# Moving background steps: modulation around layer norm 0 on TensorE, table work behind the key activations, context job at one and two steps by turns

## The chip, the cores and the metric

The kernel runs on one core of a Trainium2 chip. The metric is the device time in microseconds (us) of one execution. A core has five engines, each with its own in-order queue: TensorE (PE, with its weight loads shown as PEld), VectorE (DVE), ScalarE (ACT), GpSimd (POOL) and SyncE (SP), which issues nearly all of the loads here. The engines wait for one another, and for DMA transfers, through semaphores.

## The reference

Two blocks follow each other on an activation of 256 tokens by 2048 features, all in float32. The first block has two layers. Layer 0 is a differential attention, layer 1 a forgetting attention with its own key/value projection; after each comes `x = layer_norm(ALPHA * x + gate * y)`. The input of each projection is modulated:

```
mod = c_act @ w_mod[l] + b_mod[l]
shift, scale, gate = jnp.split(mod, 3, axis=-1)
h = x * (1.0 + scale[:, None]) + shift[:, None]
```

The second block normalises x, modulates it with the same kind of vectors, and runs an S5 mixer (a complex linear recurrence over time, whose initial state comes from a context sequence of 256 tokens), a gated linear unit, and an MLP with a hidden size of 8192. The modulation vectors are products of one vector (for one of them two vectors) with large matrices: 224 chunks of 256 rows by 1024 columns, 1 MB each, every one read once.

## The kernel before, in words

**The projections.** x is held transposed, 16 tiles of 128 features by 256 tokens. A projection is a sequence of output tiles; `weights()` (L143) hands out the weights of one tile. Each tile is 1 MB, loaded by SP in two halves (L129), and split into a high and a low fp32r part by ACT (`wh`, L133) and DVE (`wl`, L134). `mm_t` (L152) and `mm_n` (L187) then run 48 matmuls: high by high, high by low, low by high. The high and low parts have five buffers each (`HL`), so that two and a half tiles can stand ready.

**Work in the background.** Each call of `weights()` also advances two kinds of other work.

- `bg()` (L292) takes the next chunk of the modulation queue `bgq`. It issues the two loads of the chunk (`graw`, L267, four buffers of 0.5 MB shared with the context's `wc` tiles and others) and runs the use of the chunk before it (`LATE = 1`). A use is either 8 matmuls on PE (L221) or two multiply-adds of 1024 columns on DVE (L236; the first one of an accumulation is an ACT multiply, L234). Which engine, or none, is read from a cyclic policy set for the stage (`P_ON0`, `P_KV` and so on); the two-vector chunks of `mc` always run on PE. After eight chunks a half of a vector is finished (L245 to L256). The queue's order is fixed by `JOBS`: m0, m02, mk, m1, mc, m12, m22, m24, m25.
- `step()` (L272) advances the first generator of `self.side` by one step, `next(self.steps)` times a call. Three such generators exist: the S5 input table, in layer 0; `s5_outputs_table` (L598), in the key/value stage, with two steps for each of 16 blocks; and `ctx_states` (L1297), which computes the final S5 state of the context in 8 blocks of five steps, after one step of preparation. The output table's first half-step makes products on DVE (L553, L554, L634, L636) and stores them; the second runs small matmuls (`kps`, L648) that need the loaded tile `gen_ws<-d_b` (L624). A context block has 128 small matmuls (`inc`, L695) and a scan of six levels on DVE (L1353 to L1356).

**The stages around the change.** Output projection 0 (`out_norm`, L1030) runs 16 tiles. After each, ACT multiplies by the gate (`yg`, L1089) and DVE adds the residual (L1090). From the tenth tile on, shifted copies (L1061), their squares (ACT, L1063) and sums on POOL (L1065 to L1068) gather the statistics; the last ones are summed by PE (L369). DVE then takes the root (L1108 to L1114), PE spreads mean and root over the partitions (L342). `layer1` (L1136) follows: `affine_split` (L411) walks through the 16 tiles of x; `norm(j)` is an add and a multiply on DVE (L1130, L1131), ACT applies scale and shift (L416) and makes the high part (`kH`, L418), DVE the low part (`kL`, L419). Directly behind it stand six modulation chunks (`BG_K`). The key/value stage then runs 32 tiles (keys: `mm_t`, copied out at L1201; values: `mm_n`), with the forget gate's small projection after the first. The query/gate stage runs two tiles for each of 16 heads, with the attention in between; from the fifth head on the context job runs beside it, and goes on in output projection 1. Behind that, `s5_mix` first completes the accumulation that DVE has open (`while self.open`, one chunk at a time), and then starts the S5 mixer.

**What sets the order.** The program text gives priorities. A planner (`schedule_with_timeline_sim`) goes through a modelled timeline and lays down each engine's order, ahead of the run: an instruction of later text is put before one of earlier text if its operands are there sooner in that model. At run time each engine follows its list. `issue_after(ins)` places the instructions of the block that are on the engine of `ins` behind `ins` in that list; those of other engines it leaves free.

Of the kernel before, what the change touches and what calls it, by code (L numbers as in the profile page):

```python
# [49 lines left out]
KO_K = 12  # L50
P_START = ("pe",)
P_L0A = ('dve', 'pe')
P_KV = ('dve', 'pe')
P_QG = ('dve', 'dve', 'pe')
P_W = ("pe",)
P_GLU = ('dve',)
P_MLP = ('dve', None, None)
P_ON0 = ('dve', 'dve', 'dve', None)
P_ON1 = ('pe', 'dve', None)
BG_V = 2  # L60
BG_W = 0
# [4 lines left out]
LATE = 1  # L66
NPJ = 4
INC = ('pj', 'pj')
BG_K = 6
BG_Q = 0  # L70
P_CTX = (1,)
HL = 5
JOBS = ("m0", "m02", "mk", "m1", "mc", "m12", "m22", "m24", "m25")
DVE_W = 2
# [7 lines left out]
E_K = "x"  # L82
# [23 lines left out]
class K:  # L106
# [164 lines left out]

    def step(self):  # L272

        while self.side and next(self.side[0], True):
            self.side.pop(0)

    def flush(self, job):
        while job in self.side:
# [132 lines left out]
    def affine_split(self, src, S, B, dst, js=range(KT)):  # L411

        nc = self.nc
        for j in js:
            u = self.tmp("u")
            nc.scalar.activation(u, src(j), AF.Identity, scale=S[:, j:j + 1], bias=B[:, j:j + 1])  # L416
            aH, aL = dst(j)
            nc.scalar.copy(aH, u)  # L418
            nc.vector.tensor_sub(aL, u, aH)  # L419

    def pair(self, name):
        H, L = self.act_tile(F32R, name + "H"), self.act_tile(F32R, name + "L")
# [278 lines left out]
    def run(self):  # L701
        tc, I = self.tc, self.I
        from contextlib import ExitStack
        with ExitStack() as es:
# [23 lines left out]
            self.steps = itertools.cycle((1,))  # L728
            self.open = False
            self.side = []  # L730
            self.x = xr.tile([128, KT, T], F32, name="xres")
            mod = lambda n: self.vt.tile([128, KT], F32, name=n)
            self.m0 = [mod(f"m0_{i}") for i in range(3)]
# [41 lines left out]
    def V(self, n):  # L775
        i = VEC[n] * KT
        return self.vecs[:, i:i + KT]
# [109 lines left out]
    def layer0(self):  # L887
# [114 lines left out]
        self.ctx_rms()  # L1002
        self.policy(P_ON0, X_ON0)
        self.norm = self.out_norm(o_, m0[2], 0)
# [131 lines left out]
    def layer1(self):  # L1136
        nc, V = self.nc, self.V
# [2 lines left out]
            self.bg_finish(n)  # L1140
        S, B = self.small_bg("lk", V("lg0"), self.mk[1], V("lb0"), self.mk[0])
        k_ = self.pair("k")
        self.affine_split(self.norm, S, B, k_)
        self.bg(BG_K, E_K)
        Fs = self.cp.tile([48, T], F32R, name="Fs")
        nid = self.cp.tile([48, 16], F32R, name="nid")
        FT = self.cp.tile([128, 2, 16], F32, name="FT")
# [1 line left out]
        def forget():  # L1149


            wz = self.t1.tile([128, KT, 16], F32, name="wz", tag="t1")
            nc.gpsimd.dma_start(wz, self.I["wz"])
            wzH = self.t1.tile([128, KT, 16], F32R, name="wzH", tag="t1")
            wzL = self.t1.tile([128, KT, 16], F32R, name="wzL", tag="t1")
            nc.scalar.copy(wzH, wz)
            nc.vector.tensor_sub(wzL, wz, wzH)
            zf = self.m.tile([16, T], F32, name="zf", tag="m")
            for kt in range(KT):
                aH, aL = k_(kt)  # L1160
                nc.tensor.matmul(zf, wzH[:, kt], aH, start=kt == 0, stop=False)
                nc.tensor.matmul(zf, wzH[:, kt], aL, start=False, stop=False)
                nc.tensor.matmul(zf, wzL[:, kt], aH, start=False, stop=kt == KT - 1)
            fz = self.t1.tile([16, T], F32, name="fz", tag="t1")
            fa = self.t1.tile([16, T], F32, name="fa", tag="t1")
            F = self.t1.tile([16, T], F32, name="F", tag="t1")
            nc.vector.tensor_scalar(fz, zf, self.bf[:, 0:1], None, op0=ADD)
            nc.scalar.activation(fa, fz, AF.Abs)
            nc.scalar.activation(fa, fa, AF.Tanh, scale=0.5)
            nc.vector.tensor_scalar(fa, fa, 0.5, 0.5, op0=MUL, op1=ADD)  # L1170
            nc.scalar.activation(fa, fa, AF.Ln)
            nc.vector.tensor_scalar(fz, fz, 0.0, None, op0=MIN)
            nc.vector.tensor_add(fa, fa, fz)
            nc.vector.tensor_tensor_scan(F, self.ones[:16].to_broadcast([16, T]), fa, 0.0, op0=MUL, op1=ADD)
            nc.scalar.mul(Fs, self.dm[:48, 0:T], 0.0)
            nc.scalar.copy(Fs[0:16], F)
            nc.vector.tensor_sub(Fs[32:48], F, Fs[0:16])
            nc.scalar.mul(nid, self.idn[:48, 0:16], 0.0)
            for i in (0, 32):
                nc.scalar.mul(nid[i:i + 16], self.idn[i:i + 16, i:i + 16], -1.0)  # L1180
            return F

        def forget_t(F):
            fp = self.m.tile([128, 2, 16], F32, name="fp", tag="m")
            for i in range(2):
                nc.tensor.transpose(fp[:, i], F[:, i * 128:i * 128 + 128], self.idn[:16, :16])
            nc.vector.tensor_copy(FT, fp)

        kT, v = [], []
        self.policy(P_KV, X_KV)  # L1190
        vgen = self.s5_outputs_table(self.act.tile([128, 4096], F32, name="gen2_ws", tag="act"))
        self.side.append(vgen)
        for j in range(32):
            if j == 1:
                F = forget()
            if j == 3:
                forget_t(F)
            if j < 16:
                ps = self.mm_t(k_)
                t = self.kv.tile([128, T], F32, name=f"k{j}", tag="kv")  # L1200
                with self.tc.issue_after(nc.scalar.copy(t, ps).ins):  # L1201
                    nc.scalar.activation(z[:, j], z[:, j], AF.Identity, scale=V("lg0")[:, j:j + 1],
                                         bias=V("lb0")[:, j:j + 1])
                kT.append(t)
            else:
                ps = self.mm_n(k_, j % 2)
                if j % 2:
                    for h in range(2):
                        t = self.kv.tile([128, 2, 128], F32, name=f"v{j - 17 + h}", tag="kv")
                        nc.scalar.copy(t, ps[:, :, h * 128:h * 128 + 128])  # L1210
                        v.append(t)
        self.flush(vgen)
        for i in (1, 0):
            self.bg_finish(f"m1_{i}")
        s1 = self.plus1("s1_1", self.m1[1])
# [50 lines left out]
        def start_ctx():  # L1266
            if self.ctx is None and not self.bg_open("mc_0") and not self.bg_open("mc_1"):
                Sc, Bc = self.small_bg("sc", V("mixpre"), self.mc[1], None, self.mc[0])
                self.ctx = self.ctx_states(Sc, Bc)
                self.side.append(self.ctx)  # L1270
                self.steps = itertools.cycle(P_CTX)

# [484 lines left out]
```

## Time and profile before

| | us |
|---|---|
| median of 3 runs | 2521.97 |
| lowest, highest | 2521.81, 2525.11 |
| profiled execution, its own time | 2525.04 |
| span of the profile (first to last instruction) | 2523.2 |

The page gives busy time by engine: PE 2337.6 us, DVE 1782.8, ACT 1196.4, POOL 174.5. The granted clock of PE is its share of full speed: 1.0 is 2.4 GHz, 0.5 is 1.2 GHz, a value between them is a mean over the stretch. Over the execution it was 0.95. Instructions of one engine may overlap by some tens of ns, so a sum of durations can exceed a stretch a little. In the views, a tile's name with an arrow (`out<-in`) tells what an instruction writes and reads, and what stands after `<-` behind an idle time is the event that ended it.

### The profile page before, as it was taken

The numbers are of one execution on the slowest core, as the hardware profiler recorded it, in microseconds if no ns is written. First come the engines' busy times: TensorE is split into PE (matmuls) and PEld (weight loads), VectorE is DVE, ScalarE is ACT, GpSimd is POOL, SyncE is SP. The second block draws the span as 40 slices with busy tenths as digits, with TensorE's granted clock in tenths as the row PEclk, the third lists the DMA queues.
The fourth block names the chain that finished last, engine by engine and source line by source line (L and its number), as shares of the span: only waits on it lengthen the run. The fifth ranks groups of instructions, "written<-read, shape, count | busy, mean of one in ns | idle before, by whom it ended". The sixth has DMA issues, their size and how long they took to land.

```text
span 2523.2 us, 49826 instructions
## 1 busy us (share of the span) xinstructions
PE 2337.6 (93%) x19814; PEld 2039.8 (81%) x19814; DVE 1782.8 (71%) x3357; ACT 1196.4 (47%) x2077; POOL 174.5 (7%) x255
## 2 busy tenths in 40 slices
PE   5699999999889999999998569899899999999997
PEld 1289999999778888988886457798788888888885
DVE  3278878887985555788788996897865665665655
ACT  0455445445365556555544443555544443443442
POOL 0000000000301111000000001232000000000000
PEclk8599999999889999999998779999899999999998
DMA  9999999887879998888786347997356555555652
GB/s 320 331 344 319 328 331 332 302 299 291 294 230 351 325 334 295 287 275 282 247 284 251 137 174 274 325 314 245 120 189 192 190 187 187 187 186 190 192 184 92
DMA packets 195450, 644.77 MB, mean 256 GB/s; under 512 B 32624, under 2 KB 41072, under 8 KB 194832
## 3 DMA queue, kind: packets, MB, share of 16 engines
q1 hardware_dynamic: 187744, 620.47, 71.9%
q0 software_dynamic: 7472, 21.11, 2.1%
q8 instruction: 155, 2.54, 0.4%
q14 instruction: 79, 0.65, 0.1%
HBM read 615.80 MB, written 25.69 MB: 254 GB/s over the span
## 4 chain that ended last, share of the span: by engine, by line
PE 76%; DVE 11%; DMA 8%; ACT 3%; issue 3%; SPq 0%; POOL 0%; DVEq 0%; ACTq 0%
PE pj L175 19%; PE pj L162 9%; PE pj L176 9%; PE pj L164 9%; PE pj L163 9%; DMA graw<-in_w_mod 6%; PE g L221 4%; PE pjv L199 3%; PE pjv L200 2%; PE pjv L201 2%; DVE gacc L236 2%; PE ko L1472 2%; DVE wl L134 1%; DVE scan_t L1428 1%; DVE S L1430 1%
## 5 line engine op out<-in xcount | busy, mean ns | idle before, releaser
L134 DVE TENSOR_TENSOR wl<-w,wh 128x1024 fp32r<-128x1024 f32 x631 | 779.3, 1239 | 433.5 <-ACT wh L133 421.7
L133 ACT CAST wh<-w 128x1024 fp32r<-128x1024 f32 x632 | 657.5, 1048 | 689.8 <-PE pj L175 279.9
L175 PE MATMUL pj<-h,wh 128*128 128x512 f32 x1024 | 361.9, 398 | 6.0 <-DVE h L419 4.2
L175 PE MATMUL pj<-d,wh 128*128 128x512 f32 x1024 | 358.4, 396 | 0.0
L236 DVE SCALAR_TENSOR_TENSOR gacc<-graw,csilu,gacc 128x1024 f32<-128x1024 f32 x200 | 267.8, 1339 | 42.4 <-DMA graw<-in_w_mod 37.8
L176 PE MATMUL pj<-h,wl 128*128 128x256 f32 x1024 | 287.4, 281 | 1.1 <-DVE wl L134 1.1
L176 PE MATMUL pj<-d,wl 128*128 128x256 f32 x1024 | 284.8, 279 | 0.0
L175 PEld LDWEIGHTS pj<-h,wh 128*128 128x128 f32 x1024 | 194.0, 189 | 53.4 <-issue 3.9
L175 PEld LDWEIGHTS pj<-d,wh 128*128 128x128 f32 x1024 | 191.9, 188 | 47.2 <-PE pj L176 1.7
L162 PE MATMUL pj<-hH,wh 128*128 128x256 f32 x768 | 221.4, 289 | 5.4 <-ACT hH L418 4.0
L164 PE MATMUL pj<-hH,wl 128*128 128x256 f32 x768 | 221.3, 289 | 0.5 <-DVE wl L134 0.5
L163 PE MATMUL pj<-hL,wh 128*128 128x256 f32 x768 | 221.0, 288 | 0.0
L221 PE MATMUL g<-graw,czc 128*32 128x256 f32 x1840 | 170.0, 451 | 46.3 <-DMA graw<-in_w_mod 43.9
L176 PEld LDWEIGHTS pj<-h,wl 128*128 128x128 f32 x1024 | 194.7, 190 | 1.5 <-DVE wl L134 1.5
L176 PEld LDWEIGHTS pj<-d,wl 128*128 128x128 f32 x1024 | 192.8, 188 | 0.4
L162 PEld LDWEIGHTS pj<-hH,wh 128*128 128x128 f32 x768 | 148.8, 194 | 8.9 <-ACT hH L418 4.1
L164 PEld LDWEIGHTS pj<-hH,wl 128*128 128x128 f32 x768 | 148.6, 194 | 4.5 <-issue 3.3
L163 PEld LDWEIGHTS pj<-hL,wh 128*128 128x128 f32 x768 | 148.8, 194 | 3.8 <-issue 3.7
L162 PE MATMUL pj<-h1H,wh 128*128 128x256 f32 x512 | 147.1, 290 | 1.4 <-DVE ws L1286 1.4
L163 PE MATMUL pj<-h1L,wh 128*128 128x256 f32 x512 | 146.3, 287 | 0.0
L164 PE MATMUL pj<-h1H,wl 128*128 128x256 f32 x512 | 145.4, 285 | 0.0
L221 PEld LDWEIGHTS g<-graw,czc 128*32 128x32 f32 x1840 | 48.8, 117 | 119.4 <-DMA graw<-in_w_mod 92.4
(483 smaller groups left out, 5120.5 us busy)
## 6 DMA issues: line engine op xcount, KB each, us to landing
graw<-in_w_mod SPq DMA_DIRECT2D x384, 512.0 KB, 6.1
w<-in_mlp_in SPq DMA_DIRECT2D x128, 512.0 KB, 3.7
w<-in_mlp_out SPq DMA_DIRECT2D x128, 512.0 KB, 3.9
w<-in_a_in SPq DMA_DIRECT2D x96, 512.0 KB, 6.1
graw<-in_w_kvmod SPq DMA_DIRECT2D x64, 512.0 KB, 6.1
w<-in_b_in SPq DMA_DIRECT2D x64, 512.0 KB, 5.9
w<-in_glu SPq DMA_DIRECT2D x56, 512.0 KB, 6.0
w<-in_a_v SPq DMA_DIRECT2D x32, 512.0 KB, 5.9
```

The source lines that it names most:

```text
L133: nc.scalar.copy(h, src)
L134: (eng or (nc.gpsimd if next(self.spl) else nc.vector)).tensor_sub(l, src, h)
L162: self.nc.tensor.matmul(ps, h, aH, start=kt == order[0] and not opened, stop=False)
L163: self.nc.tensor.matmul(ps, h, aL, start=False, stop=False)
L164: self.nc.tensor.matmul(ps, l, aH, start=False, stop=kt == order[-1] and last)
L175: self.nc.tensor.matmul(ps, h, view(aH, 0, [[T, 2], [1, T]]), start=kt == order[0], stop=False)
L176: self.nc.tensor.matmul(ps[:, 0], l, aH, start=False, stop=kt == order[-1])
L199: self.nc.tensor.matmul(ps[:, i], aH[:, s], h, start=half == 0 and i == 0 and k == 0, stop=False)
L200: self.nc.tensor.matmul(ps[:, i], aH[:, s], l, start=False, stop=False)
L201: self.nc.tensor.matmul(ps[:, i], aL[:, s], h, start=False, stop=half == 1 and i == 1 and k == 7)
L221: nc.tensor.matmul(st["g"][32 * q:32 * q + 32], self.cz[c][:, ch * 2 + s], raw[s][:, q * 256:q * 256 + 256], start=st["n"] == 0, stop=ch = ...
L236: nc.vector.scalar_tensor_tensor(acc, raw[s], cc, acc, op0=MUL, op1=ADD)
```

## The change

Seven edits, in three parts:

- `P_ON0` no longer asks for a chunk in the last four of the 16 tiles of output projection 0 (three DVE chunks fewer there). `bg(BG_K, ...)` moves ahead of `affine_split`, with eight chunks instead of six, and all of them on PE instead of DVE. `P_KV` starts with PE instead of DVE.
- `affine_split` returns its last instruction, the DVE subtraction that makes the last `kL`. While `self.after` holds it, every step of the output table traces its instructions behind it. The table joins the side work at the second tile of the key/value stage instead of the first, and gets two steps at every eighth call (`P_VT`).
- `P_CTX` gives the context job one and two steps by turns.

Counted through the queue, the total number of chunks up to the end of the key/value stage falls by one, and one chunk more is left for each later place, up to the loop that closes the open accumulation in `s5_mix`: it runs four chunks instead of three.

```diff
--- before.py
+++ after.py
@@ -50,12 +50,13 @@
 KO_K = 12
 P_START = ("pe",)
 P_L0A = ('dve', 'pe')
-P_KV = ('dve', 'pe')
+P_KV = ('pe', 'dve')
+P_VT = (1, 1, 1, 1, 1, 1, 1, 2)
 P_QG = ('dve', 'dve', 'pe')
 P_W = ("pe",)
 P_GLU = ('dve',)
 P_MLP = ('dve', None, None)
-P_ON0 = ('dve', 'dve', 'dve', None)
+P_ON0 = ('dve', 'dve', 'dve', None) * 3 + (None,) * 4
 P_ON1 = ('pe', 'dve', None)
 BG_V = 2
 BG_W = 0
@@ -66,9 +67,9 @@
 LATE = 1
 NPJ = 4
 INC = ('pj', 'pj')
-BG_K = 6
+BG_K = 8
 BG_Q = 0
-P_CTX = (1,)
+P_CTX = (1, 2)
 HL = 5
 JOBS = ("m0", "m02", "mk", "m1", "mc", "m12", "m22", "m24", "m25")
 DVE_W = 2
@@ -271,8 +272,9 @@
 
     def step(self):
 
-        while self.side and next(self.side[0], True):
-            self.side.pop(0)
+        with self.tc.issue_after(self.after) if self.after else nullcontext():
+            while self.side and next(self.side[0], True):
+                self.side.pop(0)
 
     def flush(self, job):
         while job in self.side:
@@ -416,7 +418,8 @@
             nc.scalar.activation(u, src(j), AF.Identity, scale=S[:, j:j + 1], bias=B[:, j:j + 1])
             aH, aL = dst(j)
             nc.scalar.copy(aH, u)
-            nc.vector.tensor_sub(aL, u, aH)
+            last = nc.vector.tensor_sub(aL, u, aH).ins
+        return last
 
     def pair(self, name):
         H, L = self.act_tile(F32R, name + "H"), self.act_tile(F32R, name + "L")
@@ -728,6 +731,7 @@
             self.steps = itertools.cycle((1,))
             self.open = False
             self.side = []
+            self.after = None
             self.x = xr.tile([128, KT, T], F32, name="xres")
             mod = lambda n: self.vt.tile([128, KT], F32, name=n)
             self.m0 = [mod(f"m0_{i}") for i in range(3)]
@@ -1140,8 +1144,8 @@
             self.bg_finish(n)
         S, B = self.small_bg("lk", V("lg0"), self.mk[1], V("lb0"), self.mk[0])
         k_ = self.pair("k")
-        self.affine_split(self.norm, S, B, k_)
-        self.bg(BG_K, E_K)
+        self.bg(BG_K, "pe")
+        self.after = self.affine_split(self.norm, S, B, k_)
         Fs = self.cp.tile([48, T], F32R, name="Fs")
         nid = self.cp.tile([48, 16], F32R, name="nid")
         FT = self.cp.tile([128, 2, 16], F32, name="FT")
@@ -1189,9 +1193,10 @@
         kT, v = [], []
         self.policy(P_KV, X_KV)
         vgen = self.s5_outputs_table(self.act.tile([128, 4096], F32, name="gen2_ws", tag="act"))
-        self.side.append(vgen)
         for j in range(32):
             if j == 1:
+                self.side.append(vgen)
+                self.steps = itertools.cycle(P_VT)
                 F = forget()
             if j == 3:
                 forget_t(F)
@@ -1210,6 +1215,8 @@
                         nc.scalar.copy(t, ps[:, :, h * 128:h * 128 + 128])
                         v.append(t)
         self.flush(vgen)
+        self.steps = itertools.cycle((1,))
+        self.after = None
         for i in (1, 0):
             self.bg_finish(f"m1_{i}")
         s1 = self.plus1("s1_1", self.m1[1])
```

## Rows read from the trace of the kernel before

**Rows 1.** The page, part 1: busy us (share of the span) and instructions by engine.
```profile
PE 2337.6 (93%) x19814; PEld 2039.8 (81%) x19814; DVE 1782.8 (71%) x3357; ACT 1196.4 (47%) x2077; POOL 174.5 (7%) x255
```
**Rows 2.** Windows: stretch, length, busy us of PE, PEld, DVE, ACT, POOL; PEclk, DMA share, GB/s.
```profile
676.60:694.00 17.40, 8.51 (x37) 3.59 (x38) 15.49 (x26) 2.93 (x5) 2.32 (x9) 0.50 0.84 295
694.00:732.00 38.00, 31.69 (x175) 28.34 (x176) 36.97 (x73) 22.42 (x44) 1.65 (x3) 0.69 0.72 227
734.00:960.00 226.00, 225.39 (x2376) 195.50 (x2375) 134.48 (x188) 128.05 (x244) 39.01 (x86) 1.00 0.94 325
1060.80:1253.00 192.20, 186.09 (x1903) 168.75 (x1900) 160.73 (x301) 103.22 (x218) 2.09 (x6) 0.99 0.81 272
1253.00:1362.00 109.00, 107.61 (x1190) 92.03 (x1189) 83.87 (x141) 45.76 (x78) 4.23 (x7) 1.00 0.81 274
63.00:126.00 63.00, 42.06 (x304) 15.99 (x304) 14.97 (x45) 30.03 (x80) 0.71 (x4) 0.55 0.91 331
```
**Rows 3.** Groups of DVE, 644 to 694: busy us, mean ns, idle before and its releaser.
```profile
L236 DVE SCALAR_TENSOR_TENSOR gacc<-graw,csilu,gacc 128x1024 f32<-128x1024 f32 x15 | 24.3, 1622 | 0.6 <-ACT gacc L234 0.6
```
**Rows 4.** Timeline of PE, 673 to 693: start, us, instruction, idle before and its releaser.
```profile
673.49 0.28 PE L164 MATMUL pj<-o,wl 128*128 128x256 f32 x1
...
677.65 1.02 PE L369 MATMUL st<-zacc,ones 128*1 128x256 f32 x4 [1.60 <-POOL zacc L1068]
...
685.27 1.02 PE L369 MATMUL st<-xres,ones 128*1 128x256 f32 x4 [3.86 <-DVE xres L1061]
...
687.98 1.02 PE L379 MATMUL sums<-sel_ln,sumst 128*128 128x6 f32 x4 [0.46 <-ACT sumst L376]
...
692.70 1.22 PE L342 MATMUL lnb<-idn,mr 128*128 128x128 f32 x4 [2.22 <-DVE mr L1114]
```
**Rows 5.** Timeline of ACT and DVE, 679 to 740.
```profile
679.71 0.63 ACT L1063 ACTIVATE zsq<-xres 128x512 f32<-128x512 f32 x1 [3.97 <-DVE xres L1061]
...
694.02 0.42 DVE L1130 TENSOR_TENSOR xres<-xres,lnb 128x256 f32<-128x256 f32 x1 [0.20 <-PE lnb L342]
...
739.02 0.37 ACT L1201 COPY k<-pj 128x256 f32<-128x256 f32 x1
```
**Rows 6.** Groups of DVE, 694 to 732.
```profile
L236 DVE SCALAR_TENSOR_TENSOR gacc<-graw,csilu,gacc 128x1024 f32<-128x1024 f32 x7 | 8.9, 1276 | 0.0
L1131 DVE TENSOR_TENSOR xres<-xres,lnb 128x256 f32<-128x256 f32 x16 | 6.6, 412 | 0.1
...
L134 DVE TENSOR_TENSOR wl<-w,wh 128x1024 fp32r<-128x1024 f32 x4 | 4.9, 1215 | 0.0
L553 DVE TENSOR_TENSOR vprod<-gen_ws 128x512 f32<-128x512 f32 x4 | 2.7, 681 | 0.0
```
**Rows 7.** The chain that ended last, in order of time: start, us, what.
```profile
104.20 1.13 PE g L221 x8
...
721.20 0.21 PE pj L162
...
760.75 8.82 DMA gen_ws<-d_b
...
770.84 1.00 PE g L221 x16
...
949.89 0.12 PE pjv L200
...
1097.18 1.09 PE inc L695 x64
```
**Rows 8.** Groups of DVE, 1061 to 1253, and one row of waits, 1060 to 1252.
```profile
L236 DVE SCALAR_TENSOR_TENSOR gacc<-graw,csilu,gacc 128x1024 f32<-128x1024 f32 x25 | 32.0, 1281 | 20.4 <-DMA graw<-in_w_mod 20.2
L1356 DVE TENSOR_TENSOR ctx_ws<-ctx_ws 128x512 f32<-128x512 f32 (+4 forms) x34 | 15.3, 450 | 0.5
...
DVE gacc L236 <- DMA graw<-in_w_mod: 21.1, 12, 3.1
```
**Rows 9.** The chain that ended last, at layer norm 1.
```profile
1372.27 1.19 DVE gacc L236
```

## The prediction

> **What bounds the kernel now.** I read the page first: PE is busy for 93% of the span, DVE for 71% [rows 1]. A gain must therefore come from a stretch in which PE starves or runs at its lower clock, so I next asked for busy time by stage [rows 2]. The reader is to see two kinds of stage there. In the key/value stage (734 to 960), the heads of the query/gate stage (1060.8 to 1253) and output projection 1 (1253 to 1362) PE is busy nearly throughout at a granted clock of 0.99 to 1.00: what is moved there is paid in PE time, or hidden beside it. Around layer norm 0 (676.6 to 732) PE is busy 40.2 of 55.4 us, at 0.50 and 0.69 of full clock, and DVE 52.5 of 55.4: DVE bounds it. Time saved there passes through the key/value stage unchanged, since PE has 0.6 of 226 us free in it.
>
> Then I looked at what DVE does around the norm. From 644 to 694 it runs 15 modulation steps, 24.3 us [rows 3]. The last matmul of output projection 0 begins at 673.49, yet the first norm step starts at 694.02; PE stands before the statistics for an x that is 3.86 us late, and ACT's square before it had waited 3.97 us on DVE [rows 4, 5]. From 694 to 732 [rows 6] the keys need three groups of 16 operations like L1131's, 19.8 us. Between them lie 7 modulation steps (8.9), 12 table products (three times L553's four: 8.2) and 4 weight splits (4.9).
>
> **The change, part by part.** The profiled execution took 2525.0 us, 3.1 more than the median of 2522.0 over the three runs; I sum against the former and take 3.1 off.
>
> *Output projection 0 and the norm.* Three chunks of two loads leave the last four tiles, and the eight after the norm go to PE, ahead of the key activations. Of the 15 DVE steps before 694 one stays: 22.7 of DVE's 50 us fall free, and it is no longer behind PE. From the last matmul's end, 673.8, follow yg, residual, shift and square, some 2.2 us (the square is 0.63 [rows 5]), then band sums, closing and selection as from 685.27 to 689.00, 3.7 us: 679.7. The root takes 689.0 to 692.7 with one step of 1.2 inside, so 2.5 without; spread to first norm step is 1.3 [rows 4, 5]. First norm step at 683.5 instead of 694.0. I take 9 of these 10.5 us, because POOL's accumulation also ends late, at 677.6 [rows 4]; it is the next thing late.
>
> *Key activations.* From the 37.6 us up to the last kL I take 5 of 7 modulation steps (6.4) and all table products (8.2). That leaves 23.0. Gain 14.6, of which I take 13.5, since more steps of the first tiles may be drawn in. Sum for the norm: **−22.5 us**. The table work is now behind the last key activation on DVE alone; its DMAs on SP and copies on ACT have no such order. Its 8.2 us fall into the key/value stage, where DVE is busy 134 of 226 us: free; without that cover it would cost 8.2.
>
> *Is PE fast enough?* Three key tiles, 144 matmuls, run as activations arrive. At the lower clock one takes 0.21 us, at the higher 0.12 [rows 7]: 30 or 17 us. Even at 0.21 from 685 on they end by 715, against a third key copy at 739.02 [rows 5]: 24 us earlier. At startup the modulation matmuls came in bursts of eight, paced by their loads, and stood at a granted clock of 0.55 (63 to 126 [rows 2, 7]), so I do not count on them to keep the clock up. The Trainium skill ("TensorE: Matmul & The Clock Gate", Part 1 on the clock gate) says that the lower clock is the default and that activity releases it. By it the new PE steps would hold the higher clock, the keys would end with DVE at 709, and this part would be −26. The startup row speaks against it.
>
> *DMA.* The eight chunks are 16 loads of 0.5 MB, 8.4 MB through four buffers. At the key/value stage's 325 GB/s [rows 2] that is 26 us; begun near 660 it ends by about 690, before the keys do. A chunk costs PE 0.5 us (1.00 for 16 matmuls), or 1.13 at the lower clock [rows 7], inside PE's gap. In order behind them on PE wait the spread and the first key tiles; on SP, weights of tile 3 and the table's loads. Were all eight put ahead of the spread, it would wait for the last load from 682 to 690, and 8 us of the norm's gain would be lost: range of this part −15 to −26.
>
> *Key/value stage.* m1's last half has five chunks on PE instead of three, one two-vector chunk fewer falls here: +0.5. The table does two steps at every eighth tile; a load of its d_b took 8.82 us on the chain [rows 7], more than a 7 us tile, so each of three doubles can hold PE for some 2 us: 0 to +6. I take **+1** for both, as PE now loses 0.6 here in all.
>
> *Context job.* Two tiles give three steps instead of two. The last 24 tiles of the query/gate stage then do 36 steps instead of 24, and the job ends in the fourth tile of output projection 1. The 24 steps cost DVE four groups of products there, each like L1356's, 59 us together [rows 8], 2.5 a step: 12 more bring 29.5, less 2.6 for one DVE chunk that slides into the next stage. DVE goes from 160.7 of 192.2 us to 187.6. PE gains 2.4 blocks of two times 64 small matmuls at 1.09 us [rows 7], +5.3, and the stage 197.5: DVE 95% busy. Its idle time before was 31.5 us, 20.4 of it before modulation steps, for their loads [rows 8]. I take 5 us of new stalls; the bounds on the stage are −3 (PE's present gaps close) and +27 (no idle is used). Output projection 1 gives back 5.3 of PE work and its 1.4 us of idle. Net 5.3 + 5 − 6.7 = **+3.6**.
>
> *Tail of layer norm 1.* One modulation chunk slides from the query stage to the loop that closes the open accumulator: four DVE chunks instead of three. Two more steps of 1.28, perhaps a load, where one such step already ends just before the first norm step [rows 9], while the context products that now stand among them leave: −3 to +4. I take **+1.7**.
>
> Sum: −22.5 + 1 + 3.6 + 1.7 = −16.2. From 2525.0 to 2508.8 in the profiled execution, **2505.7 us** as a median.
>
> **The rivals.**
> *DVE bounds the query/gate stage (slower).* For it: 95% in an in-order queue, and context weights take buffers of the same four-deep ring as the modulation loads. Against it: PE idles only 6.1 us there now. If none of DVE's idle time is used, the stage costs +27 and projection 1 returns 6.7: −22.5 + 1 + 27 − 6.7 + 1.7 = +0.5, 2522. Five more ring loads that each add the longest wait seen, 3.1 us [rows 8], make it +16: 2538. It decides once that stage is over 26 us longer, 2.2 us for each of twelve heads; then no gain is left. Middle 2530.
>
> *PE waits for modulation loads.* Step matmuls stand in front of the spread or of key tiles, and the loads pace them. For it: startup. Against: DMA was 0.84 busy from 676.6 to 694 with the old loads still among them [rows 2], so early loads find room. The norm gains only 10: 2518.
>
> *The better case.* The clock rule holds (−26), the query stage has no new stalls (5.3 − 6.7 = −1.4), the tail gains 1.3: −28.7, or 2493; with half of the stalls 2496.
>
> *The steps do not leave DVE's key stretch*, because the planner draws later ones forward as it does now: counted out by the policy, four of the seven steps after 694 belong to key tiles 0 and 2. Three DVE chunks remain in that half, five steps instead of the two that I left in: 3.8 us more, 2509.5, inside the forecast's own range.
>
> **How the numbers follow.** Forecast 0.60 (own range 2498 to 2514), PE waiting for loads 0.14, DVE-bound query stage 0.12, better case 0.14. A measurement can tell 0.2%, 5.0 us: faster is below 2517.0, slower above 2527.0. Faster: 0.58 + 0.06 + 0.02 + 0.14 = 0.80; same: 0.02 + 0.07 + 0.04 = 0.13; slower: 0.07, nearly all from the query stage. The range runs from 2494, just above the better case's end, to 2520, which takes in the loads' case and leaves out the DVE-bound stage.
>
> **What would show it.** Right: first norm step 9 us sooner after the last matmul, no table product between it and the last kL, kL done near 709, third key copy near 715, the key/value stage as long as now, the eighth context block done in the fourth tile of projection 1, PE still busy in the query stage. Wrong: key matmuls held behind modulation matmuls that wait for loads; the heads with context over 2 us longer each; PE waiting for the table at its double steps; a first norm step of layer norm 1 that starts later after the last matmul than now.

## The result and the profile after

The changed kernel takes 2545.4 us (median of 4 runs, 2542.9 to 2549.6) against 2523.2 for the kernel before, of which there are now 4 runs, too: a ratio of 1.009, 95% interval 1.0074 to 1.0106. It is 0.9% slower, where 0.6% faster was forecast; the range of 2494 to 2520 does not hold it. The profiled execution took 2547.1 us, with a span of 2545.0.

The page's part 1 of the changed kernel answers to [rows 1]. PE is busy 16 us longer and DVE 22 us shorter, and the span is 22 us longer: PE has waited more and run slower.

```profile
PE 2353.2 (92%) x19958; PEld 2043.9 (80%) x19958; DVE 1760.9 (69%) x3339; ACT 1192.7 (47%) x2077; POOL 173.0 (7%) x255
```

The table gives the length of each stretch in the two traces, from start to start of instructions that both have. "Key copy" and "v copy" are ACT's copies of finished keys and values; the first gg is the first `gg<-pj`, ahead of which four `gg<-ko` stand. The 48 small matmuls of the forget gate (`zf`, 0.12 us each) can fall on either side of the third key copy: 28 of them come before it in the kernel before, all 48 in the changed one. So a time to the third key copy compares exactly only between kernels with the same number, and the time to the last v copy compares always.

| us | before | after | difference |
|---|---|---|---|
| start to last o matmul (projection 0) | 673.5 | 671.0 | -2.5 |
| to third key copy | 65.5 | 61.3 | -4.2 |
| to last v copy (key/value stage) | 220.8 | 221.5 | +0.7 |
| to last yg (query/gate stage and projection 1) | 403.6 | 428.0 | +24.4 |
| to first scan step (layer norm 1) | 35.8 | 37.4 | +1.6 |
| to first gg (S5 stage) | 233.2 | 231.4 | -1.8 |
| to last store | 887.0 | 890.7 | +3.7 |

Two stretches decide: the one with the norm and the keys, where 22.5 us were forecast and 4.2 came (3.6 at the last v copy), and the query/gate stage with projection 1.

**The keys.** The windows of the changed kernel answer to [rows 2] (columns as there).

```profile
640.00:676.00 36.00, 33.47 (x286) 31.66 (x284) 27.08 (x25) 19.14 (x27) 20.74 (x20) 1.00 0.64 206
676.00:694.00 18.00, 11.25 (x101) 4.49 (x101) 13.30 (x43) 0.37 (x1) 0.00 (x0) 0.81 0.73 255
694.00:732.00 38.00, 35.60 (x288) 26.84 (x289) 22.98 (x39) 22.48 (x49) 1.42 (x4) 0.87 0.89 307
732.00:954.00 222.00, 220.47 (x2324) 193.42 (x2326) 133.36 (x189) 126.28 (x243) 41.38 (x86) 1.00 0.96 328
...
1060.00:1250.00 190.00, 175.86 (x1968) 155.16 (x1968) 162.54 (x318) 100.88 (x214) 0.76 (x4) 0.93 0.78 266
```

DVE is no longer the bound from 694 to 732: 23.0 us busy of 38. ACT does almost nothing before 694, and DMA, which was to be busy with early chunk loads from 660, moves only 206 GB/s up to 676. The timeline of SP's queue shows why (start, us, instruction).

```profile
641.72 2.74 SPq L268 DMA_DIRECT2D graw<-in_w_mod  x2
...
651.07 22.79 SPq L130 DMA_DIRECT2D w<-in_kv_k  x9
679.90 22.97 SPq L268 DMA_DIRECT2D graw<-in_w_mod  x15
...
706.69 6.49 SPq L268 DMA_DIRECT2D graw<-in_w_mod  x5
```

From 645 to 679.9 no chunk load is issued. The four buffers hold two chunks whose matmuls stand on PE behind the statistics and the first part of the spread. Only when these run, from 678.8 on, do the other loads start, each as a buffer comes free, and the last is issued at 704. One row of SP's waits, 640 to 715, says the same (what waits and for what: us in total, times, longest).

```profile
SPq L268 <- PE g L222: 19.3, 15, 6.0
```

The timelines of PE, ACT and DVE show what waits for the loads (idle before an instruction and its releaser in brackets).

```profile
678.76 2.79 PE L222 MATMUL g<-graw,czc 128*32 128x256 f32 x32
681.48 0.71 PE L344 MATMUL lnb<-idn,mr 128*128 128x128 f32 x4
683.73 0.64 PE L222 MATMUL g<-graw,czc 128*32 128x256 f32 x8 [1.53 <-DMA graw<-in_w_mod]
...
698.03 1.08 PE L222 MATMUL g<-graw,czc 128*32 128x256 f32 x8 [0.17 <-DMA graw<-in_w_mod]
...
700.03 0.37 ACT L249 COPY gs<-g 128x256 f32<-128x256 f32 x1 [23.38 <-PE g L246]
700.30 2.57 ACT L418 ACTIVATE u<-xres,lkb,lks 128x256 f32<-128x256 f32 x5
...
703.19 1.44 DVE L421 TENSOR_TENSOR kL<-u,kH 128x256 fp32r<-128x256 f32 x4 [8.23 <-ACT kH L420]
...
704.12 0.75 PE L163 MATMUL pj<-kH,wh 128*128 128x256 f32 x3
```

The last matmul of the spread starts at 681.9, and the norm steps of the 16 tiles run from 682.3 to 695.0, as forecast. But the first key activation starts at 700.30. In ACT's list the copy `gs` of the modulation half that these chunks finish stands ahead of it, and ACT waits 23.4 us for it, some 17 of them after the first tile of x is ready (683.2). On PE the key matmuls stand behind the chunks as well.

**The query/gate stage.** Two rows of waits for each kernel, from the last v copy to the last yg: first before, then after (columns as in SP's row).

```profile
PE tp L1250 <- ACT ws L1245: 3.2, 2, 1.9
DVE gacc L236 <- DMA graw<-in_w_mod: 34.7, 21, 3.1
```

```profile
PE tp L1257 <- ACT ws L1252: 9.6, 6, 5.3
PE pv L1262 <- ACT ws L1258: 3.9, 2, 3.3
...
DVE gacc L237 <- DMA graw<-in_w_mod: 41.1, 20, 6.0
```

PE waits for the attention's weights (`ws`), which wait for DVE. The longest wait, 5.3 us up to 1058.2, can be followed back: DVE stands for 2.2 us before a modulation step whose load is late, the reciprocal of the attention comes behind that step and a weight split, and ACT waits for the reciprocal.

```profile
1055.20 1.28 DVE L237 SCALAR_TENSOR_TENSOR gacc<-graw,csilu,gacc 128x1024 f32<-128x1024 f32 x1 [2.23 <-DMA graw<-in_w_mod]
...
1057.53 0.16 DVE L1249 RECIPROCAL sr<-se 128x2 f32<-128x2 f32 x1
...
1057.73 0.80 ACT L1252 ACTIVATE ws<-ws,sr 128x128 f32<-128x128 f32 x2 [3.70 <-DVE sr L1249]
```

PE does nearly the same work in this stretch in both traces (1024 `inc`, 1536 `h1` and 768 projection 1 matmuls; 370 chunk and closing matmuls after 342), so I summed the time from start to start by kind of matmul. PE's idle time (in steps of over 0.6 us, what goes beyond a normal step) grows from 8.3 to 22.7 us; the `h1` matmuls take 2.7 us longer, the chunks 3.3, `inc` 2.0, scores and the rest some 2. Part of what is not idle time is the clock. Windows of the changed kernel around the same wait:

```profile
1040.00:1052.00 12.00, 12.00 (x150) 11.41 (x150) 11.36 (x18) 2.87 (x8) 0.00 (x0) 1.00 0.86 263
1052.00:1056.00 4.00, 0.92 (x8) 0.71 (x6) 1.77 (x3) 2.02 (x5) 0.00 (x0) 1.00 0.84 330
1056.00:1062.80 6.80, 4.62 (x28) 3.13 (x28) 6.80 (x10) 5.07 (x13) 0.00 (x0) 0.50 0.66 230
```

PE, busy before, stands nearly still for 4 us, and its granted clock is then 0.50 for 6.8. From 1060 to 1250 the mean is 0.93; before it was 0.99.

### The profile page after: what moved, and what is told of

The parts are those of the page before. It is cut to its first block, busy times and chain, and to the rows that moved or that the text cites. A ratio compares the mean times of both kernels' runs of the same rounds, so it can differ in the third digit from the quotient of the medians.

```text
span 2545.0 us, 50094 instructions
## 1 busy us (share of the span) xinstructions
PE 2353.2 (92%) x19958; PEld 2043.9 (80%) x19958; DVE 1760.9 (69%) x3339; ACT 1192.7 (47%) x2077; POOL 173.0 (7%) x255
## 4 chain that ended last, share of the span: by engine, by line
PE 80%; DVE 8%; DMA 8%; ACT 2%; issue 2%; SPq 0%; DVEq 0%; POOL 0%; ACTq 0%
PE pj L176 18%; PE pj L163 10%; PE pj L164 10%; PE pj L165 10%; PE pj L177 9%; DMA graw<-in_w_mod 6%; PE g L222 4%; PE pjv L200 3%; PE pjv L201 2%; PE pjv L202 2%; PE ko L1479 2%; DVE gacc L237 1%; DVE wl L135 1%; PE y L1508 1%; DVE scan_t L1435 1%
## 5 line engine op out<-in xcount | busy, mean ns | idle before, releaser
L237 DVE SCALAR_TENSOR_TENSOR gacc<-graw,csilu,gacc 128x1024 f32<-128x1024 f32 x182 | 240.9, 1324 | 53.4 <-DMA graw<-in_w_mod 46.6
L222 PE MATMUL g<-graw,czc 128*32 128x256 f32 x1984 | 186.8, 465 | 52.0 <-DMA graw<-in_w_mod 49.9
```

Of the source, the lines that this page charges most:

```text
L222: nc.tensor.matmul(st["g"][32 * q:32 * q + 32], self.cz[c][:, ch * 2 + s], raw[s][:, q * 256:q * 256 + 256], start=st["n"] == 0, stop=ch = ...
L237: nc.vector.scalar_tensor_tensor(acc, raw[s], cc, acc, op0=MUL, op1=ADD)
```

## The experiments

Stretches as in the table above. Every length is from one execution, and executions of one kernel scatter (20 of the kernel before in one session: 2515.1 to 2530.6), so a few us of a length mean little; medians and ratios are of timed runs. The two need not agree: the profiled execution was the longest of all runs in no_ctx, mod_only, tab_only, early4 and early4_vt1 (3.9 to 9.2 us above their medians), and the shortest in ctx_only (4.8 below). Each ratio is to the kernel before as timed in the same session.

| kernel | last o to third k | to last v | to last yg | to first scan step | to first gg | to end | median | ratio to before (95%) |
|---|---|---|---|---|---|---|---|---|
| before | 65.5 | 220.8 | 403.6 | 35.8 | 233.2 | 887.0 | | |
| after | 61.3 | 221.5 | 428.0 | 37.4 | 231.4 | 890.7 | 2545.4 | 1.0074-1.0106 |
| ctx_only | 65.4 | 220.2 | 426.6 | 35.5 | 222.0 | 888.8 | 2541.3 | 1.0067-1.0104 |
| no_ctx | 64.0 | 222.5 | 409.8 | 38.0 | 221.2 | 886.3 | 2516.0 | 0.9967-0.9986 |
| mod_only | 64.4 | 217.0 | 412.1 | 38.3 | 226.6 | 888.4 | 2519.6 | 0.9978-0.9998 |
| tab_only | 67.5 | 215.6 | 410.5 | 36.0 | 234.4 | 887.9 | 2524.7 | 1.0003-1.0026 |
| pe_behind | 57.1 | 222.5 | 418.4 | 36.8 | 225.2 | 886.9 | 2522.2 | 0.9994-1.0013 |
| nomod | 47.7 | 209.0 | 413.0 | 65.6 | 235.2 | 896.5 | 2539.8 | 1.0054-1.0090 |
| early4 | 45.5 | 232.0 | 410.9 | 36.8 | 227.2 | 885.0 | 2512.1 | 0.9954-0.9980 |
| early4_notab | 57.2 | 224.4 | 413.2 | 37.6 | 226.1 | 891.4 | 2529.4 | 1.0028-1.0060 |
| early4_vt1 | 46.7 | 229.4 | 406.1 | 36.8 | 234.0 | 888.0 | 2513.7 | 0.9961-0.9983 |
| qg_pe | 65.6 | 221.6 | 410.5 | 35.3 | 223.3 | 887.1 | 2521.9 | 0.9987-1.0010 |
| ctx_qg_pe | 65.6 | 221.0 | 425.1 | 34.5 | 222.5 | 888.7 | 2531.3 | 1.0020-1.0047 |
| ctx112 | 61.6 | 223.3 | 423.9 | 36.3 | 232.9 | 886.0 | 2541.4 | 1.0077-1.0106 |
| rg5 | 58.9 | 225.6 | 414.2 | 34.6 | 232.4 | 892.7 | 2536.1 | 1.0040-1.0082 |
| rg5_noctx | 58.4 | 223.0 | 405.1 | 39.3 | 232.9 | 895.8 | 2531.2 | 1.0032-1.0069 |
| scan_z2 | 65.6 | 220.1 | 402.0 | 35.0 | 235.7 | 888.7 | 2524.9 | 1.0009-1.0030 |

### Which part costs

**ctx_only**, the kernel before with one line changed, and **no_ctx**, the changed kernel with that line undone:

```diff
-P_CTX = (1,)
+P_CTX = (1, 2)
```

> Kernel before with the third part alone: the context job at one and two steps by turns. Theory A (the context job's extra steps lengthen the query/gate stage by themselves): first to last pv goes from 253 to 275 to 278 us, projection 1 returns nothing, 2541 to 2548 us. Rival B (the stage grew because the two other parts change which modulation chunks fall into it): alone the steps cost 0 to 8, first to last pv at most 261, 2523 to 2531 us.

> Changed kernel with the third part undone (one context step per tile). Theory A: first to last pv is back at 253 with 4 us of play, the 6 to 7 us that were gained up to the first pv stay, the tail of layer norm 1 costs 1 to 2: 2515 to 2520 us. Rival B (the stage is longer for the other two parts' sake): at least 2535 us.

Theory A holds. The context's steps alone cost 23.0 us in the stretch with the query/gate stage; without them the changed kernel is there at 409.8, 18.2 less. But no_ctx does not gain where it was to: its last yg comes later than in the kernel before (its three stretches sum to 696.3, before's to 689.9), so its total in the range of theory A is luck. Its whole gain lies in the S5 stage, 12.0 us shorter, which the change does not touch. The 6.2 us that no_ctx, too, takes longer from the last v copy to the last yg go, as far as one execution of each can tell, with the two other parts: 28 chunk matmuls of the trace more, 1.9 us of idle time more, and slower `h1` and `inc` matmuls.

**mod_only** is the kernel before with the edits of `P_ON0`, `P_KV` and `BG_K` and the moved `bg(BG_K, "pe")`; **tab_only** has the rest without `P_CTX` (`issue_after`, the later start, `P_VT`).

> Kernel before with the modulation part alone; the table's work may go where the planner likes. Theory (the key phase waits for modulation loads, so DVE has room there and the table's place is worth nothing): third key copy at 732 with 2 us of play, as in the changed kernel, and 2515 to 2521 us. Rival (the 8 us of table products on DVE still count): the last kL is some 8 us later, third key copy near 740, 2523 to 2528 us.

> Kernel before with the second part alone: the output table's steps behind the last key subtraction, begun at the second tile, two steps at every eighth. Theory (DVE bounds the key phase of the kernel before, where 12 table products took 8.2 us): third key copy 5 to 8 us sooner after the last o matmul than 65.5, the key/value stage 0 to 4 longer, S5 stage in the order of the kernel before; 2516 to 2521 us. Rival (what the key phase gains goes into waits for the table's loads): last o matmul to last v copy stays within 2 of 286.3; 2521 to 2526 us.

In mod_only the third key copy comes 64.4 us after the last o matmul, as in no_ctx: with the keys held by the chunks the table's place is worth nothing there. (By the clock of the span it comes at 736.8, not at 732; the total is in the theory's range.) In tab_only DVE is rid of the table products and the last kL does come 4.6 us sooner (726.6 against 731.2), but the third key copy does not. At the last v copy 3.2 us of gain are left, and 6.9 are lost behind it; 0.15% slower in all. That is the rival's total, though the 283.1 us to the last v copy are just outside the 2 us that it allowed. Neither part brings more than 0.12% on its own.

### What holds the keys

**pe_behind**, no_ctx with

```diff
-        self.bg(BG_K, "pe")
         self.after = self.affine_split(self.norm, S, B, k_)
+        self.bg(BG_K, "pe")
```

> Changed kernel with one context step per tile, and with the eight PE chunks behind the key activations in the text instead of ahead of them. That takes the closing copy of the finished half (gs) from the head of ACT's key activations to their end, and puts chunk matmuls among the key matmuls on PE. Theory 1 (ACT's queue behind that copy is what held the keys): first kL within 2.5 us of the first norm step, last kL near 703, third key copy near 717, 2501 to 2507 us. Theory 2 (the loads of the eight chunks are the bound, through PE's order as well): kL as in theory 1, but the last of the chunks' loads still lands between 706 and 712, PE waits for them among the key tiles, third key copy at 727 to 732, 2513 to 2520 us.

**nomod**, no_ctx with `BG_K = 0`:

> Changed kernel with one context step per tile and no modulation chunk at the keys at all (the eight fall later). Theory (the chunks' loads pace the keys, through PE's order and through ACT's): PE goes from the spread to the key matmuls, first kL within 2.5 us of the first norm step, last kL near 700, third key copy at 706 to 714, over 20 us sooner than with the eight chunks. Rival (without modulation matmuls the clock stays at its lower level and paces the keys instead): third key copy at 720 to 726. In all 2512 to 2530 us, since eight chunks more fall later, and the S5 stage has the order of the kernel before.

**early4**, no_ctx with

```diff
-P_ON0 = ('dve', 'dve', 'dve', None) * 3 + (None,) * 4
+P_ON0 = ('dve', 'dve', 'dve', None) * 3 + ('pe',) * 4
-BG_K = 8
+BG_K = 4
```

> Changed kernel with one context step per tile, four of the eight PE chunks moved into the last four tiles of output projection 0. Theory (loads pace the keys): half of the loads run beside the projection, last o matmul to third key copy falls from 64 to 48 to 56 us, 2503 to 2513 us. Rival (the four load buffers are not free any sooner, so the loads move by nothing): 62 us or more, 2514 to 2520 us.

In pe_behind the first kL follows the spread after 2.4 us instead of 21.1: ACT's wait is gone, and with it 6.9 us up to the third key copy. The rest of the wait is still there, since chunks now stand among the key matmuls. So ACT's queue was one hold, PE's order behind the same loads the other. For the third key copy theory 2 was right (728.9); the total, 2522, missed both, since 8.6 us more than in no_ctx go by between last v copy and last yg. Without chunks (nomod) the first kL comes as the theory said, the last at 704.4 instead of near 700, and the third key copy 16.3 us sooner than in no_ctx, at 718.4: between the theory's time and the rival's. The rival's reason holds for the smaller part only, as nomod's windows show:

```profile
676.00:689.60 13.60, 9.63 (x40) 8.65 (x41) 9.70 (x35) 7.06 (x18) 0.00 (x0) 0.50 0.18 54
689.60:719.00 29.40, 29.16 (x262) 25.66 (x262) 25.13 (x48) 19.58 (x38) 1.11 (x2) 1.00 0.54 175
```

Up to 689.6 27 key matmuls go at 0.21 us a step, at 0.50 of full clock; at the later 0.12 they would have taken 2.4 us less. From 689.6 on the keys' own matmuls have the full clock, and PE is busy throughout: the keys' matmuls themselves are the bound then. The chunks did not bring the clock up: in no_ctx PE is busy for three quarters of the time from 689.6 to 710, nearly all with chunks, at half clock.

```profile
689.60:710.00 20.40, 15.37 (x112) 5.08 (x113) 10.81 (x30) 6.29 (x16) 0.86 (x3) 0.50 0.89 305
```

The eight chunks that nomod leaves out come back later: layer norm 1 takes 30 us more, and it ends 0.7% slower, at 2539.8 against the 2512 to 2530 expected. early4 keeps them and moves half of their loads into the projection. SP's queue in early4:

```profile
655.16 0.80 SPq L268 DMA_DIRECT2D graw<-in_w_mod  x2
...
662.31 0.90 SPq L268 DMA_DIRECT2D graw<-in_w_mod  x2
...
669.04 0.80 SPq L268 DMA_DIRECT2D graw<-in_w_mod  x2
...
676.82 0.80 SPq L268 DMA_DIRECT2D graw<-in_w_mod  x2
...
678.20 15.33 SPq L268 DMA_DIRECT2D graw<-in_w_mod  x7
```

Loads run all the while, and the last o matmul to third key copy falls to 45.5 us: 20.0 less than before, 18.5 less than in no_ctx. But all 48 matmuls of the forget gate come behind that copy here, and all 48 before it in no_ctx: 5.8 of the 18.5 us are only this move. The other 12.7, with the same eight chunks, show that the place of the loads was the hold. The kernel is 0.33% faster than before, 1.2% faster than the changed one, and, with early4_vt1, the best of this study. Of the 18.5 us, 9.5 are given back in the key/value stage: the forget gate's matmuls and the like add 5.6 there and idle time of PE 5.0, in several short waits, and the others take 1.1 less. At the last v copy 9.0 are left against no_ctx and 8.8 against before. How much of the 0.33% comes from the keys is left open, though: in the profiled execution the last yg comes at 1363.6, where it came before (1363.4), and what is gained in all lies behind it, 6.0 of it in the S5 stage; in that of early4_vt1, below, the last yg comes 4.9 us sooner (1358.5).

**early4_vt1** (`P_VT = (1,)`) and **early4_notab** (the table part undone) ask what the table does to that:

> The kernel with four PE chunks in the last four tiles of projection 0 and four at the keys, with the table at one step per tile throughout. Theory (the double steps make PE wait for the table's loads in the key/value stage): third key copy to last v copy falls from 232 to 227 to 230, and 2507 to 2511 us. Rival (that stage is held by something else): 231 to 234, 2510 to 2515 us.

> The kernel with four PE chunks in the last four tiles of projection 0 and four at the keys, with the table part undone, so modulation alone. Theory (the table part is worth the 3 to 4 us that the two kernels with and without it differed by): 2514 to 2518 us. Rival (it is worth nothing here, since the keys now wait for nothing on DVE): 2510 to 2513 us; last o matmul to third key copy 44 to 50 in both.

The double steps are worth 2.6 us of that stage at most, as the theory said (229.4), and the time does not change (2513.7, the rival's range). Without the table part the keys need 57.2 instead of 45.5 us. DVE's groups of early4_notab, 690 to 725:

```profile
L236 DVE SCALAR_TENSOR_TENSOR gacc<-graw,csilu,gacc 128x1024 f32<-128x1024 f32 x5 | 6.4, 1281 | 0.0
...
L553 DVE TENSOR_TENSOR vprod<-gen_ws 128x512 f32<-128x512 f32 x4 | 2.8, 688 | 0.4 <-DMA gen_ws<-d_l 0.4
L554 DVE TENSOR_TENSOR vprod<-gen_ws 128x512 f32<-128x512 f32 x4 | 2.7, 685 | 0.0
L636 DVE TENSOR_TENSOR gen_ws<-vprod 128x512 f32<-128x512 f32 x2 | 1.4, 686 | 0.0
L634 DVE TENSOR_TENSOR gen_ws<-vprod 128x512 f32<-128x512 f32 x2 | 1.4, 685 | 0.0
```

Here are the 12 table products, 8.3 us, and two chunk steps more than in early4. So the prediction's 8.2 us for them were right, once nothing else holds the keys. Both expectations for the total missed (2529.4): the table part, worth nothing alone, is worth 17 us of the medians here. The two profiled executions differ by 10.9 only: 11.7 at the keys, of which 4.2 are left at the last v copy, and 6.4 after the first gg, which I did not follow. Where the rest of the 17 lies no trace shows.

### What the context's steps cost

**qg_pe**, the kernel before with `P_QG = ('pe',)`, and **ctx_qg_pe**, the same with `P_CTX = (1, 2)`:

> Kernel before with every background chunk of the query/gate stage on PE (none on DVE). A control for the next kernel: 38 multiply-adds (48 us) leave DVE there, 19 chunks of 8 matmuls come to PE, 0.7 us each. Last v copy to last yg of projection 1: from 404 to 410 to 418 us; 2523 to 2537 us, less what the planner's order of the S5 stage may give back (here it starts its outputs earlier among the scans, as in the three kernels that took 249 to 256 us there instead of 260).

> The same, with the context job at one and two steps by turns. Theory D (the extra steps cost 20 us because DVE's queue is overfull and the attention waits in it): with DVE relieved by 48 us the steps cost little, last v copy to last yg within 6 us of the control. Rival P (the cost is in the context's own matmuls and their copies, on PE and ACT): 18 to 24 us above the control, with PE's idle time in the stage still near 22 us.

The control is as expected in this stretch (410.5). The steps cost 14.6 us here, with 42 us of DVE work gone: neither theory. PE's idle time grows from 2 to some 12 us, and what PE waits for has changed. First qg_pe, then ctx_qg_pe:

```profile
PE inc L695 <- DMA wc<-d_w: 1.7, 1, 1.7
```

```profile
PE inc L695 <- DMA wc<-d_w: 6.4, 6, 2.1
PE tp L1250 <- ACT ws L1245: 1.5, 2, 1.0
```

The attention is nearly in time; now the context's own weights are late. They use the ring of four buffers that the modulation chunks use. **ctx112** has `P_CTX = (1, 1, 2)`:

> Changed kernel with the context job at one, one and two steps by turns: a third of the extra steps. Theory D in its linear form (each extra step costs): last v copy to last yg 5 to 8 above the 409.8 of one step per tile, S5 stage in the order of the kernel before (231 to 235): 2529 to 2535 us. Rival (a threshold: DVE has room for a third of them): within 3 of 409.8, 2523 to 2528 us.

My expectation miscounted: 8 of 24 tiles have a double step instead of 12, two thirds of the extra steps, not a third. The cost is 14.1 us against 18.2, or 1.8 and 1.5 us for each double tile: no sign of a threshold, though both expectations missed the total (2541.4). **rg5** and **rg5_noctx** are after and no_ctx with

```diff
-            self.rg = pool("rg", 4)
+            self.rg = pool("rg", 5)
```

> Changed kernel with five instead of four buffers of 0.5 MB in the ring that modulation chunks and context weights share. Ring theory (late loads at the head of DVE's queue are what the extra context steps cost): DVE's waits for chunk loads between last v copy and last yg, 41.1 us, fall by over 10, and that stretch from 428 to 420 or less; 2530 to 2538 us. Queue theory (the products of the extra steps themselves stand in front of the attention): within 4 of 428, even where the waits fall; 2540 to 2548 us. At the keys one more load can start ahead of the norm: last o matmul to third key copy 57 to 60 instead of 61.3.

> The control: five buffers, one context step per tile. Last v copy to last yg 405 to 410 us. The extra steps' cost is the difference between this kernel and the one before it in that stretch: 10 us or less by the ring theory, 15 to 21 by the queue theory. S5 stage in the order of the kernel before: 2519 to 2527 us in all.

Waits in the stretch, first rg5, then rg5_noctx:

```profile
DVE gacc L237 <- DMA graw<-in_w_mod: 29.7, 21, 3.2
...
PE tp L1257 <- ACT ws L1252: 4.2, 4, 1.8
```

```profile
DVE gacc L237 <- DMA graw<-in_w_mod: 37.2, 19, 4.4
...
PE tp L1257 <- ACT ws L1252: 6.1, 5, 2.2
```

Every number that the ring theory gave for the changed kernel came. One buffer more takes 11.4 us off DVE's waits for loads and 13.8 off the stretch (3.2 and 4.7 without the extra steps); the extra steps now cost 9.1 us there instead of 18.2, and 4.9 in the medians (29.4 with four buffers, where the S5 stages differ by 10.2, too). PE's idle time is 9.6 and 9.7 us with and without them. So half of the cost goes with the fifth buffer. The other half remains as slower matmuls. The way from the buffer to PE is seen in the longest wait of the changed kernel, above, but it is not shown for the whole: DVE's waits for loads do not follow the cost. The same row, first for ctx_only, where the extra steps cost 23.0 us and the kernel before had 34.7, then for no_ctx, which lacks the steps and waits as long as the changed kernel:

```profile
DVE gacc L236 <- DMA graw<-in_w_mod: 28.9, 18, 4.3
```

```profile
DVE gacc L237 <- DMA graw<-in_w_mod: 40.4, 22, 4.7
```

What counts is which wait has the attention behind it, and this was not summed. In ctx_only and ctx112 PE also waits once for one of ACT's copies for the context (`ctx_ws`), 3.8 and 6.3 us. Both kernels with five buffers lose elsewhere, and rg5_noctx missed its total (2531.2 instead of 2519 to 2527): behind the first gg they take 2.0 and 9.5 us longer than after and no_ctx, and rg5_noctx has the longer S5 stage; neither was followed.

### The S5 stage

Its length from first scan step to first gg is 231 to 235 us in seven kernels (before, after, tab_only, nomod, ctx112, both with five buffers) and 221 to 227 in eight, without a change to it in any of these. In DVE's order the first output (`z`) stands behind 166 to 168 of the 252 scan steps (`S<-scan_t`) in the former, and behind 144 to 157 in the latter. **scan_z2** tries to move only that, in the kernel before:

```diff
-                for i in range(len(segs)):
+                for i in ((len(segs) - 1,) if n else range(len(segs) - 1)):
...
-                    with self.tc.issue_after(ends[i - 2]) if i > 1 else nullcontext():
+                    with self.tc.issue_after(zlast if n else ends[i - 2]) if i > 1 else nullcontext():
```

(`if n == 0` becomes `if n in (0, 2)`, `zlast` is the last output of the block before.)

> Kernel before with one thing changed in the S5 stage, far from the change: the fourth of its scans is placed on DVE behind the second block of outputs, so that outputs stand earlier among the scan steps. Theory S (the planner's order in that stage is worth 6 to 11 us by itself, and the changes upstream only tip it): first scan step to first gg falls from 233 to 221 to 228, 2511 to 2517 us. Rival (the stage is shorter in those kernels for another reason, such as loads that ran ahead): 230 to 235, 2519 to 2525 us.

The rival is the nearer one (235.7): the outputs came earlier (behind 161), the tail after the scans shrank by 19 us, the scans grew by 22. And early4_vt1, whose outputs stand early (behind 153), took 234.0 in its profiled run, 9 us above that kernel's median. So what shortens this stage is not shown, only that a change far ahead of it can move it by 10 us. The changed kernel and the kernel before have the same length there, so it plays no part in the result; in the profiled executions of no_ctx and early4 it is most of the gain or more.

## Why the prediction was wrong

- **First norm step 9 us sooner**: right, 11.7 sooner by the clock of the span, or 9.2 after the last o matmul.
- **Key activations, 13.5**: the step that failed first. DVE was freed as counted (23.0 us busy), but the sum held only DVE's work. The sentence "begun near 660 it ends by about 690" was wrong: the four buffers were taken from 645 on, and none came free before PE had passed the statistics, at 678.8. I had named what waits on PE behind a late load, but had not asked what ACT's list has behind the chunks: the closing copy of a finished half. The rival "PE waits for modulation loads" was the true one, and at 4.2 us of gain instead of 10 its price was too kind.
- **"A chunk costs PE 0.5 us"**: mis-sized. The 920 chunk matmuls of the kernel before are 1840 in the trace, so a chunk is 16 of the trace's matmuls, 1.00 us by its own row in [rows 7]; 264 more matmuls of chunks and their closing in qg_pe took 17.3 us, 1.05 for 16.
- **The clock**: not to count on the chunks was right, as no_ctx's window shows. The Trainium skill ("TensorE: Matmul & The Clock Gate", Part 1) has the lower clock as the default that activity releases; the trace agrees for the key matmuls (nomod, 0.50 and then 1.00), and shows no release by the chunk matmuls of no_ctx (15.4 of 20.4 us busy, 0.50).
- **Key/value stage +1**: +0.7. The tail of layer norm 1, +1.7: +1.6. Both right in sign and size; that they fit to 0.3 us is luck, since single executions scatter by more.
- **Context job +3.6**: the large miss, +24.4 together with projection 1, of which 18.2 go with the steps. Two terms failed. "I take 5 us of new stalls": idle time grew by 14.4, and the clock fell after the long waits. DVE's 18.9 us of waiting for loads from 1053 to 1271 stayed nearly what it was in [rows 8] (20.2), as in the rival that lets none of the idle time be used; the stage from first to last pv grew by 23.6 against that rival's 27. And "projection 1 gives back 6.7" gave back nothing: before, 130 of its matmuls had run ahead of the last pv, in the holes of the attention, and now 45 do; 85 at 0.12 us are the 10 us that ate the saving.
- **The chances**: the two rivals were held to exclude each other and the forecast. They came together, and four load buffers have a part in both: the keys waited for them, and half of the context steps' cost in its stretch went with a fifth.

## What to carry to other kernels

Work that is moved from one engine to another keeps its loads. Before counting the engine time, count the buffers: where the last reader of a buffer is placed sets when the next load starts, and a ring shared by two jobs makes each wait for the other. When a step is moved ahead of others, follow every engine that it touches to its last instruction; a closing copy on a third engine, in order, can hold what the move was to free. And compare an upstream change stage by stage, since a stage far behind can shift by more than the change is worth.

## What the runs showed that was not expected

- After some 4 us in which PE stands nearly still its granted clock is 0.50 for the next 6.8 us (1052 to 1063 above), so such a wait costs more than its length.
- PE busy 15.4 of 20.4 us with chunk matmuls in groups of eight, each behind a load, stayed at 0.50 of full clock.
- A fifth buffer of 0.5 MB shortened a stretch that PE seemed to bound by 13.8 us with the extra context steps, and by 4.7 without them.
- Two parts that bring next to nothing apart (mod_only -0.12%, tab_only +0.15%) bring 0.33% together once the loads are early, though how much of that comes from the keys is open.
